# Delta-rule layer: decay exponents spread over partitions by DMA instead of matmuls, and a new order of exponentials and projections

## The chip, the cores and the metric

The kernel runs on one core of a Trainium2 chip. TensorE (matmuls), VectorE, ScalarE and GpSimd (called POOL in the profile) each run their own in-order queue of instructions; SyncE (SP) only issues transfers here. The metric is the device time of one execution in microseconds, the median of several runs.

## What is computed

An encoder trunk over 512 positions of width 1024: a gated delta-rule mixer, an MLP, a gated linear attention mixer and an MLP, each followed by a layer norm. The change lies in the first mixer alone. For each of 8 heads and both directions it does, in chunks (cut from the reference):

```python
gc = jnp.cumsum(g.reshape(bn, h, n, CHUNK), axis=-1)
decay_mat = jnp.exp(jnp.where(causal, gc[..., :, None] - gc[..., None, :], -jnp.inf))
a_mat = jnp.where(strict, jnp.einsum('bhncd,bhnsd->bhncs', kb, k) * decay_mat, 0.0)
lhs = a_mat + jnp.eye(CHUNK, dtype=F32)
sol = lax.linalg.triangular_solve(lhs, rhs, left_side=True, lower=True, unit_diagonal=True)
u, w = sol[..., :dv], sol[..., dv:]
qk = jnp.einsum('bhncd,bhnsd->bhncs', q, k) * decay_mat
q_dec = q * jnp.exp(gc)[..., None]
...
v_new = u_c - jnp.einsum('bhcd,bhde->bhce', w_c, state)
o = jnp.einsum('bhcd,bhde->bhce', qd_c, state) + jnp.einsum('bhcs,bhse->bhce', qk_c, v_new)
state = state * gl_c[..., None, None] + jnp.einsum('bhcd,bhce->bhde', kd_c, v_new)
```

Here `g` is the log decay of each position, `gc` its running sum. The matrix `decay_mat` needs, for each pair of positions, the exponential of a difference of two running sums: one varies along the partitions, the other along the free axis.

## The kernel before, in words

The kernel works in chunks of 128 positions, 4 per head (`NT`), with 2 directions, so a head has 8 matrices of 128x128. It splits float32 operands in two halves for the projections (`mm3`, lines 128 to 130: three matmuls of 512 columns per 128 rows of depth, 24 per block, four blocks k, q, v, z per head).

The layer is written as generators of one head each, `project`, `rows`, `solve`, `recur` and `finish`, and the loop in `gdn` (line 1367) runs through them: in step i it traces the recurrence of head i-2, the solve of head i-1, the projection of head i, then the finish of head i-2. The order in which they are traced gives each instruction its priority. A planner then works out the order on each engine ahead of time: it takes ready instructions by priority, with a cost for each, and gives out buffers as they come free. So the next head's projection fills the gaps of the current head's solve. `issue_after(x)` puts what follows behind x on x's engine, and `in_order` fixes an order by hand.

The steps that matter here:

- `project` (line 1423) loads and splits the weights (`wcols`, `split`, lines 102 and 107: a cast on ScalarE, a subtraction on VectorE), multiplies, and convolves on ScalarE and VectorE (`conv`, line 1408: a scaling and four shifted multiply-adds). After k and q it takes SiLU of both and calls `rows`.
- `rows` (line 1463) transposes k and q to get the norms, and forms for each position `rw`, its running log decay less half the log of k's norm (line 1488). It splits `rw` in three bfloat16 parts (1492 to 1496), transposes them in four matmuls into 6 rows (`rtp`, 1499), and copies these to SBUF (`rt`, 1501).
- `solve` (line 1519) multiplies k with itself (`kk`, 1528). Two matmuls with a 0/1 matrix `sel` (1534) put the rows, summed over their three parts, on all 128 partitions in two PSUM banks (`ep`); ScalarE takes their exponential times q (`qd`, 1536 and 1537). Two more matmuls add a triangular mask of -1e30 (`mi`, 1549) to the same banks. ScalarE takes `exp(ep + cj)`, 8 pieces per head (`E`, 1553), and VectorE multiplies by `kk` (1555). From there on the triangular inverse is built by doubling block sizes 4 to 64 (`xp`, 1585; `lv`, 1614 to 1634). The last copies of the inverse are on ScalarE (`Dd`, 1649) and VectorE (1651); a correction step and the products of `E` with q and k (`qke`, 1674) end the solve.
- `recur` (line 1687) runs through the 4 chunks of both directions and forms the output with `qd` and `qke` (1744). `finish` normalises it.
- The masks are built once at the start by POOL (`masks`, line 1170), after the gates.

SBUF tiles come from rings: `E` has two buffers of 2 KB per partition, `qd` four; PSUM has two banks for `ac` (where `ep` and all matrices of the solve go), three for `pj` (projections), two for `ch` and one for `tp`.

Of the kernel before, what the change touches and what calls it, by code (L numbers as in the profile page):

```python
# [8 lines left out]
F32 = mybir.dt.float32  # L9
# [8 lines left out]
P = 128  # L18
# [1103 lines left out]
class GdnConst:  # L1122


    def __init__(self, c, pool, w_in, w_g, a_log, dt_bias, conv_w, norm_g, x):
        self.c, self.pool = c, pool
        nc = c.nc
# [42 lines left out]
    def masks(self):  # L1170
        c, pool = self.c, self.pool
        G = c.nc.gpsimd
        self.idb = pool.tile([P, P], BF16, name="idb", bufs=1)
        G.tensor_copy(self.idb, c.ident)
        self.idh = pool.tile([P, P], F16, name="idh", bufs=1)
        G.tensor_copy(self.idh, c.ident)

        sf = pool.tile([6, 2, P], F32, name="self", tag="E", bufs=2)
        G.memset(sf, 0.0)
        for s in range(3):  # L1180
            G.affine_select(out=sf, in_=sf, compare_op=ALU.not_equal, fill=1.0, base=-2 * s,
                            pattern=[[-1, 2], [0, P]], channel_multiplier=1)
        self.sel = pool.tile([6, 2, P], BF16, name="sel", bufs=1)
        G.tensor_copy(self.sel, sf)
        self.mi = [pool.tile([P, P], BF16, name=f"mi{d}", bufs=1) for d in range(2)]
        for d in range(2):
            t = pool.tile([P, P], F32, name="tri", tag="cf", bufs=2)
            self.tri(t, d, False, 0.0, NEG)
            G.tensor_copy(self.mi[d], t)

# [146 lines left out]
def gdn(c, w_in, conv_w, a_log, dt_bias, norm_g, w_out, ln_g, ln_b, x, xt, w_next):  # L1337
    tc, nc = c.tc, c.nc
    w_in, w_g = w_in
    with c.banks(ch=2, pj=3, tp=1, ac=2), tc.tile_pool(name="gdn", bufs=1) as pool:  # L1340
        g = GdnConst(c, pool, w_in, w_g, a_log, dt_bias, conv_w, norm_g, xt)
        hi = [c.big.tile([P, 2, S], F32R, name=f"oh{t}", tag=f"xt{t}") for t in range(NT)]
# [8 lines left out]
        def load_z(hf):  # L1351
            if hf:
                tl = pool.tile([P, NT, S], F32, name="z", tag="sil", bufs=3)
            else:
                tl = heads[-1].next.kq
                more = [heads[-1].t2(tag, n).rearrange("p n i -> p (n i)") for tag, n in (("kt", 3), ("qd", 4))]
            for t in range(NT):
                z[t][hf] = tl[:, t, :] if hf or t < 2 else more[t - 2]
                c.dma(z[t][hf], x[t * P:(t + 1) * P, 512 * hf:512 * hf + 512])
# [7 lines left out]
        for i in range(A_H + 2):  # L1367
            old, mid, new = (heads[j] if 0 <= j < A_H else None for j in (i - 2, i - 1, i))
            if old:
                run(old.recur(done))  # L1370
            if mid:
                run(mid.solve(done))
            if new:
                run(new.project(done))
            if i >= A_H:
                load_z(i - A_H)
                run(c.out_pieces(w_out, early, lhs, z, "pj", (i - A_H,), 1))
            if old:
                run(old.finish(done))
# [7 lines left out]
class GdnHead:  # L1387
# [20 lines left out]
    def conv(self, a, ps, ci):  # L1408

        V, A, g = self.c.nc.vector, self.c.nc.scalar, self.g  # L1410
        A.mul(a, ps, g.cw[:, 2, ci:ci + 1])
        for k in (0, 1, 3, 4):
            d = k - 2
            lo, hi = max(0, -d), S - max(0, d)
            V.scalar_tensor_tensor(a[:, lo:hi], ps[:, lo + d:hi + d], g.cw[:, k, ci:ci + 1], a[:, lo:hi],
                                   ALU.mult, ALU.add)

    def new_tile(self):
        self.sil = self.pool.tile([P, 4, S], F32, name="sil", tag="sil", bufs=3)
        self.kq = self.sil[:, 2:4, :]  # L1420
        return self.sil[:, 0:2, :]

    def project(self, done):
# [6 lines left out]
        for i, ci in enumerate((A_H + h, h, 2 * A_H + h, 3 * A_H + h)):  # L1430
# [16 lines left out]
            if i < 3:  # L1447
                self.conv(kq[:, i, :] if i < 2 else self.v, ps, ci)
            else:
                A.copy(self.sz, ps)  # L1450
            if i == 1 or i == 3 and h == A_H - 1:
                t = vz if i == 3 else self.sil if h else kq
                c.exp_ln_after(A.activation(t, t, AF.Silu))
            yield 0.69, 0.0
            if i == 1:
                rows = self.rows(done)
                if h:
                    yield from rows
                else:
# [3 lines left out]
    def rows(self, done):  # L1463
# [20 lines left out]

        rw = c.small.tile([P, NT, 2], F32, name="rw", tag="rw")
        self.cj = cj = c.small.tile([P, NT, 2], F32, name="cj", tag="cj")
        lnk = lnr[:, 0, :].unsqueeze(2).to_broadcast([P, NT, 2])
        V.scalar_tensor_tensor(rw, lnk, -0.5, g.gc[:, :, :, h], ALU.mult, ALU.add)

        rs = c.small.tile([P, NT, 6], BF16, name="rsp", tag="rsp")  # L1490
        r1 = c.small.tile([P, NT, 2], F32, name="r1", tag="r1")
        V.tensor_copy(rs[:, :, 0:2], rw)
        V.tensor_tensor(r1, rw, rs[:, :, 0:2], ALU.subtract)
        V.tensor_copy(rs[:, :, 2:4], r1)
        V.tensor_tensor(r1, r1, rs[:, :, 2:4], ALU.subtract)
        V.tensor_copy(rs[:, :, 4:6], r1)
        rtp = self.bank("rtp", BF16, tag="tp")
        for n in range(NT):
            T.transpose(rtp[:6, n, :], rs[:, n, :], g.idb)
        self.rt = pool.tile([6, S], BF16, name="rt", tag="rt", bufs=2)  # L1500
        A.copy(self.rt, rtp[:6, :, :].rearrange("p n i -> p (n i)"))
        V.scalar_tensor_tensor(cj, lnk, -0.5, g.lg[:, :, :, h], ALU.mult, ALU.add)
# [16 lines left out]
    def solve(self, done):  # L1519
# [10 lines left out]

        eps, self.qd = [], []
        for d in range(2):
            ps = self.bank("ep")
            T.matmul(ps, g.sel[:, d, :], self.rt, start=True, stop=True)
            x = self.t2("qd", 4)
            A.activation(x, ps, AF.Exp)
            V.tensor_tensor(x, self.kq[:, 1, :].rearrange("p (n i) -> p n i", n=NT), x, ALU.mult)
            self.qd.append(x)
            eps.append(ps)
        yield 0.63, 1.4  # L1540

        ath, atl = t8("ath", 1), t8("atl", 1)
# [3 lines left out]
        ex, ats = [], []  # L1546
        with c.in_order(mybir.EngineType.PE):
            for d in (1, 0):
                T.matmul(eps[d], g.idb, g.mi[d].unsqueeze(1).to_broadcast([P, NT, P]), start=False, stop=True, skip_group_check=True)
        for d, ps in enumerate(eps):  # L1550
            e = self.t2("E", 2)
            for n in range(NT):
                A.activation(e[:, n, :], ps[:, n, :], AF.Exp, bias=self.cj[:, n, d:d + 1])
            at = kks if d else self.t2("on", 2)
# [31 lines left out]
        xd = t8("Xd", 1)  # L1586
        A.copy(xd, xp)

# [59 lines left out]
        for d in range(2):  # L1648
            A.copy(dd[row(1 - d), dirs[d], row(d)], ps[row(1 - d), d, :, :])
        for d in range(2):  # L1650
# [36 lines left out]
    def recur(self, done):  # L1687
# [52 lines left out]
        for n in (1, 2, 0, 3):  # L1740
            mm = [(self.qke[d][:, n, :], vns[d][n]) for d in range(2)]
            mm += [(self.qd[d][:, n, :], states[d][n]) for d in range(2) if states[d][n] is not None]
            for i, (l, r) in enumerate(mm):
# [102 lines left out]
```

## Time and profile before

| | |
|---|---|
| median of 3 runs | 1328.03 us (1326.8 to 1328.38) |
| the profiled execution | 1328.52 us |
| its span in the trace | 1326.6 us |
| mean granted TensorE clock | 0.997 of full |
| TensorE, VectorE, ScalarE, POOL busy | 1307.4, 1107.7, 805.2, 124.8 us |
| instructions | 22309 |

The delta-rule layer is the first of four and takes about the first 420 us. Durations of matmuls include the time in which they overlap with the next one, so two instructions of 0.39 us may start 0.23 us apart. In rows of a timeline the first column is the start from the beginning of the span, the second the duration, and equal instructions in a row are merged, with their count behind an x.

### The profile page before, as it was taken

Reading aid. Unit: us, or ns where it says so; the run is one execution under the profiler, and the core shown is the slowest. Engines: PE = TensorE matmul, PEld = TensorE weight load, DVE = VectorE, ACT = ScalarE, POOL = GpSimd, SP = SyncE. Lnnn points to the kernel's source line nnn. Section 1 sums busy time; section 2 is a strip of 40 time slices with the busy share of each in tenths; the row PEclk is TensorE's granted clock in tenths of the full one; section 3 lists DMA queues with packets and bytes.
Section 4 is the critical chain, followed back from the end, with each engine's and each line's share of the span. In section 5 each row is a group of like instructions: output and inputs, shape, how many; then the busy total and the mean of one; then the engine's idle time right before and its main releaser. Section 6 shows DMA issues by size and latency. Waiting matters only on the chain.

```text
span 1326.6 us, 22309 instructions
## 1 busy us (share of the span) xinstructions
PE 1307.4 (99%) x8659; PEld 1113.2 (84%) x8659; DVE 1107.7 (83%) x1823; ACT 805.2 (61%) x1598; POOL 124.8 (9%) x177
## 2 busy tenths in 40 slices
PE   9999999999999999999999999999999999999996
PEld 7777877787777889999998888888889889999985
DVE  7787888888668988989988787967879789989887
ACT  4757666767643666566667754654456466666656
POOL 5000000000000910101102200000001001101021
PEclk9999999999999999999999999999999999999998
DMA  5210120211222585675648521111216465657465
GB/s 181 96 49 33 49 65 33 64 49 57 73 99 85 189 178 154 156 191 153 151 150 170 149 90 64 65 63 64 95 64 213 105 193 154 149 172 161 142 143 143
DMA packets 44045, 154.36 MB, mean 116 GB/s; under 512 B 5419, under 2 KB 5795, under 8 KB 43939
## 3 DMA queue, kind: packets, MB, share of 16 engines
q1 hardware_dynamic: 32163, 110.85, 24.9%
q0 software_dynamic: 11776, 42.08, 16.1%
q8 instruction: 68, 1.11, 0.3%
q14 instruction: 38, 0.31, 0.1%
HBM read 113.99 MB, written 2.10 MB: 88 GB/s over the span
## 4 chain that ended last, share of the span: by engine, by line
PE 92%; ACT 3%; DVE 3%; issue 1%; DVEq 0%; POOL 0%; ACTq 0%; POOLq 0%
PE fx L128 3%; PE fx L130 3%; PE fx L129 3%; PE pX L130 3%; PE pX L129 3%; PE pX L128 3%; PE pjv L128 3%; PE pjv L129 3%; PE pjv L130 3%; PE m L1708 3%; PE fyz L128 3%; PE fyz L129 3%; PE fyz L130 3%; PE pY L129 2%; PE pY L128 2%; PE pY L130 2%
## 5 line engine op out<-in xcount | busy, mean ns | idle before, releaser
L102 ACT CAST wh<-wst 128x1024 fp32r<-128x1024 f32 x152 | 159.4, 1049 | 110.3 <-PE fyz L129 35.3
L107 DVE TENSOR_TENSOR wl<-wst,wh 128x1024 fp32r<-128x1024 f32 x150 | 184.3, 1229 | 42.2 <-ACT wh L102 41.9
L107 DVE TENSOR_TENSOR w2l<-w2r,w2h 128x1024 fp32r<-128x1024 f32 x92 | 112.3, 1221 | 24.0 <-ACT w2h L102 23.8
L102 ACT CAST w2h<-w2r 128x1024 fp32r<-128x1024 f32 x94 | 98.5, 1048 | 47.4 <-PE pX L130 16.2
L415 POOL DMA_DIRECT2D w2r<-w2r x56 | 48.5, 892 | 493.9 <-DVE w2l L107 247.3
L102 ACT CAST ah<-h 128x1024 fp32r<-128x1024 f32 x56 | 58.9, 1052 | 40.8 <-PE pX L129 18.1
L464 DVE TENSOR_TENSOR wst<-wst 128x512 f32<-128x512 f32 x120 | 79.8, 685 | 0.4
L107 DVE TENSOR_TENSOR al<-h,ah 128x1024 fp32r<-128x1024 f32 x56 | 68.3, 1220 | 5.1 <-ACT ah L102 4.8
L130 PE MATMUL pX<-w2h,al 128*128 128x512 f32 x168 | 66.2, 394 | 0.0
L129 PE MATMUL pX<-w2l,ah 128*128 128x512 f32 x168 | 66.1, 393 | 0.0
L128 PE MATMUL pX<-w2h,ah 128*128 128x512 f32 x168 | 65.8, 392 | 0.0
L128 PE MATMUL pjv<-wh,xth 128*128 128x512 f32 x128 | 54.7, 427 | 0.0
L128 PE MATMUL fx<-xth,wh 128*128 128x256 f32 x192 | 53.6, 279 | 0.0
L130 PE MATMUL fx<-xh,wl 128*128 128x256 f32 x192 | 53.6, 279 | 0.0
L130 PE MATMUL fyz<-xh,wl 128*128 128x256 f32 x192 | 53.6, 279 | 0.0
L128 PE MATMUL fyz<-xh,wh 128*128 128x256 f32 x192 | 53.6, 279 | 0.0
L128 PE MATMUL fx<-xh,wh 128*128 128x256 f32 x192 | 53.5, 278 | 0.0
L129 PE MATMUL fx<-xl,wh 128*128 128x256 f32 x192 | 53.5, 278 | 0.0
L130 PE MATMUL fx<-xth,wl 128*128 128x256 f32 x192 | 53.4, 278 | 0.0
L129 PE MATMUL fx<-xtl,wh 128*128 128x256 f32 x192 | 53.4, 278 | 0.0
L129 PE MATMUL fyz<-xl,wh 128*128 128x256 f32 x192 | 53.4, 278 | 0.0
L129 PE MATMUL pj<-xtl,wh 128*128 128x256 f32 (+1 forms) x160 | 52.0, 326 | 0.2 <-DVE xtl L194 0.2
(538 smaller groups left out, 4320.7 us busy)
## 6 DMA issues: line engine op xcount, KB each, us to landing
wst<-in_w SPq DMA_DIRECT2D x68, 512.0 KB, 4.3
w2r<-in_w SPq DMA_DIRECT2D x60, 512.0 KB, 4.0
w2r<-w2r POOLq DMA_DIRECT2D x56, 512.0 KB, 5.3
wst<-in_a_in SPq DMA_DIRECT2D x32, 512.0 KB, 3.3
wst<-in_b_vr SPq DMA_DIRECT2D x16, 512.0 KB, 3.3
wst<-in_a_out SPq DMA_DIRECT2D x8, 512.0 KB, 3.3
wst<-in_b_in SPq DMA_DIRECT2D x8, 512.0 KB, 3.3
wst<-in_b_out SPq DMA_DIRECT2D x8, 512.0 KB, 3.3
```

The lines of the kernel that those rows point to most:

```text
L102: h = nc.scalar.copy(hi, src)
L107: self.halves = h, nc.vector.tensor_tensor(lo, src, hi.bitcast(F32), ALU.subtract)
L128: mm(ps, ah, bh, start=start, stop=False, **kw)
L129: mm(ps, ah, bl, start=False, stop=False, **kw)
L130: self.last_mm = mm(ps, al, bh, start=False, stop=stop, **kw)
L415: nc.gpsimd.dma_start(blocks[a + (q,)], blocks[b + (q,)], accum_op=ALU.add)
L464: plus = lambda a, b: V.tensor_tensor(a, a, b, ALU.add)
L1708: T.matmul(ps[:, d, :], *ops(d), start=True, stop=True)
```

## The change

The rows are no longer spread over the partitions by matmuls. The triangular masks of both directions go to DRAM once, repeated for four chunks; for each head a transfer from SP's queue loads them into `E`. One float32 transpose turns `rw` into 8 rows of 128, a copy takes them to SBUF, a transfer from ScalarE's queue writes them to DRAM, and two transfers from POOL's queue read them back, broadcast to all partitions: one adds to `E`, one fills `qd`. ScalarE then takes both exponentials in place, from SBUF.

The exponentials of `E` are put behind a named ScalarE instruction: the last copy into `Dd` of the solve of the head before, and for head 0 the scaling at the head of head 1's q convolution. Those of `qd` come behind the copy of `xp` to `Xd`. The convolutions of k and q, SiLU and `rows` of heads 1 to 7 get a higher priority (`soon`). In step 1 of the loop the projection of head 1 is traced ahead of the solve of head 0, which gets a priority as if it began at the same point.

```diff
-    def __init__(self, c, pool, w_in, w_g, a_log, dt_bias, conv_w, norm_g, x):
+    def __init__(self, c, pool, dram, w_in, w_g, a_log, dt_bias, conv_w, norm_g, x):
...
     def masks(self):
-        self.idb = pool.tile([P, P], BF16, name="idb", bufs=1)
-        G.tensor_copy(self.idb, c.ident)
...
-        sf = pool.tile([6, 2, P], F32, name="self", tag="E", bufs=2)
-        G.memset(sf, 0.0)
-        for s in range(3):
-            G.affine_select(out=sf, in_=sf, compare_op=ALU.not_equal, fill=1.0, base=-2 * s,
-                            pattern=[[-1, 2], [0, P]], channel_multiplier=1)
-        self.sel = pool.tile([6, 2, P], BF16, name="sel", bufs=1)
-        G.tensor_copy(self.sel, sf)
-        self.mi = [pool.tile([P, P], BF16, name=f"mi{d}", bufs=1) for d in range(2)]
+        later = pool.tile([P, 2, P], F32, name="later", bufs=1)
         for d in range(2):
-            t = pool.tile([P, P], F32, name="tri", tag="cf", bufs=2)
-            self.tri(t, d, False, 0.0, NEG)
-            G.tensor_copy(self.mi[d], t)
+            self.tri(later[:, d, :], d, False, 0.0, NEG)
+        self.later = self.dram.tile([P, 2, NT, P], F32, name="laterd", bufs=1)
+        for n in range(NT):
+            G.dma_start(self.later[:, :, n, :], later)
...
+            if i == 1:
+                start = tc.cur_priority
+                run(new.project(done))
+                mid.solved = new.begun
+                with tc.high_priority(offset=tc.cur_priority - start):
+                    run(mid.solve(done))
+                continue
             if mid:
                 run(mid.solve(done))
...
+    def soon(self, n=350):
+        return self.c.tc.high_priority(offset=n) if self.h else contextlib.nullcontext()
...
             if i < 3:
-                self.conv(kq[:, i, :] if i < 2 else self.v, ps, ci)
+                with self.soon(250) if i < 2 else contextlib.nullcontext():
+                    begun = self.conv(kq[:, i, :] if i < 2 else self.v, ps, ci)
+                if i == 1:
+                    self.begun = begun
...
-                c.exp_ln_after(A.activation(t, t, AF.Silu))
+                with self.soon():
+                    c.exp_ln_after(A.activation(t, t, AF.Silu))
             yield 0.69, 0.0
             if i == 1:
+                self.e = pool.tile([P, 2, NT, P], F32, name="E", tag="E", bufs=2)
+                c.nc.sync.dma_start(self.e, g.later)
                 rows = self.rows(done)
                 if h:
-                    yield from rows
+                    with self.soon():
+                        yield from rows
...
-        rw = c.small.tile([P, NT, 2], F32, name="rw", tag="rw")
+        rdn = c.small.tile([P, 2, NT], F32, name="rw", tag="rw")
+        rw = rdn.rearrange("p d n -> p n d")
...
-        V.tensor_copy(rs[:, :, 0:2], rw)
-        V.tensor_tensor(r1, rw, rs[:, :, 0:2], ALU.subtract)
-        V.tensor_copy(rs[:, :, 2:4], r1)
-        V.tensor_tensor(r1, r1, rs[:, :, 2:4], ALU.subtract)
-        V.tensor_copy(rs[:, :, 4:6], r1)
-        rtp = self.bank("rtp", BF16, tag="tp")
-        for n in range(NT):
-            T.transpose(rtp[:6, n, :], rs[:, n, :], g.idb)
-        self.rt = pool.tile([6, S], BF16, name="rt", tag="rt", bufs=2)
-        A.copy(self.rt, rtp[:6, :, :].rearrange("p n i -> p (n i)"))
+        rtp = self.bank("rtp", shape=(2 * NT, P), tag="tp")
+        T.transpose(rtp, rdn.rearrange("p d n -> p (d n)"), c.ident)
+        rt = pool.tile([2 * NT, P], F32, name="rt", tag="rt", bufs=2)
+        A.copy(rt, rtp)
+        row = g.dram.tile([2 * NT, P], F32, name="row", tag="row", bufs=3)
+        self.qd = pool.tile([P, 2, NT, P], F32, name="qd", tag="qd", bufs=2)
+        c.nc.scalar.dma_start(row, rt)
+        every = row.rearrange("u p -> (u p)").partition_broadcast(P)
+        c.nc.gpsimd.dma_start(self.e.rearrange("p d n i -> p (d n i)"), every, accum_op=ALU.add)
+        c.nc.gpsimd.dma_start(self.qd.rearrange("p d n i -> p (d n i)"), every)
...
-        eps, self.qd = [], []
-        for d in range(2):
-            ps = self.bank("ep")
-            T.matmul(ps, g.sel[:, d, :], self.rt, start=True, stop=True)
-            x = self.t2("qd", 4)
-            A.activation(x, ps, AF.Exp)
-            V.tensor_tensor(x, self.kq[:, 1, :].rearrange("p (n i) -> p n i", n=NT), x, ALU.mult)
-            self.qd.append(x)
-            eps.append(ps)
-        yield 0.63, 1.4
...
-        with c.in_order(mybir.EngineType.PE):
-            for d in (1, 0):
-                T.matmul(eps[d], g.idb, g.mi[d].unsqueeze(1).to_broadcast([P, NT, P]), start=False, stop=True, skip_group_check=True)
-        for d, ps in enumerate(eps):
-            e = self.t2("E", 2)
-            for n in range(NT):
-                A.activation(e[:, n, :], ps[:, n, :], AF.Exp, bias=self.cj[:, n, d:d + 1])
+        for d in range(2):
+            e = self.e[:, d, :, :]
+            with c.tc.issue_after(self.solved.ins):
+                for n in range(NT):
+                    A.activation(e[:, n, :], e[:, n, :], AF.Exp, bias=self.cj[:, n, d:d + 1])
...
-        A.copy(xd, xp)
+        with c.tc.issue_after(A.copy(xd, xp).ins):
+            for d in range(2):
+                x = self.qd[:, d, :, :]
+                A.activation(x, x, AF.Exp)
+                V.tensor_tensor(x, self.kq[:, 1, :].rearrange("p (n i) -> p n i", n=NT), x, ALU.mult)
...
-            A.copy(dd[row(1 - d), dirs[d], row(d)], ps[row(1 - d), d, :, :])
+            self.next.solved = A.copy(dd[row(1 - d), dirs[d], row(d)], ps[row(1 - d), d, :, :])
```

## Rows read from the trace of the kernel before

**Rows 1.** Page, part 1: engines, busy us (share of the span) xinstructions.

```profile
PE 1307.4 (99%) x8659; PEld 1113.2 (84%) x8659; DVE 1107.7 (83%) x1823; ACT 805.2 (61%) x1598; POOL 124.8 (9%) x177
```

**Rows 2.** Table by stretches, the sum of eight stretches from 50 to 420 us.

```profile
sum 370.00, PE 366.50 PEld 288.77 DVE 300.01 ACT 233.67 POOL 2.38; mean PE 45.81 PEld 36.10 DVE 37.50 ACT 29.21 POOL 0.30
```

**Rows 3.** Timeline of TensorE, head 0: start us, us, engine, line, operation, tiles, shapes.

```profile
39.52 0.60 PE L1473 MATMUL ktp<-ident,sil 128*128 128x128 f32 x4
39.88 0.48 PE L128 MATMUL pjk<-xth,wh 128*128 128x512 f32 x1
...
43.91 0.40 PE L130 MATMUL pjk<-xth,wl 128*128 128x512 f32 x1
44.24 0.39 PE L1499 MATMUL rtp<-idb,rsp 128*6 128x128 bf16 x4
44.56 0.50 PE L128 MATMUL pjq<-xth,wh 128*128 128x512 f32 x1
44.90 0.40 PE L129 MATMUL pjq<-xtl,wh 128*128 128x512 f32 x1
...
47.05 0.60 PE L1534 MATMUL ep<-rt,sel 6*128 6x512 bf16 x2
47.58 0.50 PE L128 MATMUL pjq<-xth,wh 128*128 128x512 f32 x1
...
48.62 0.39 PE L129 MATMUL pjq<-xtl,wh 128*128 128x512 f32 x1
48.85 0.61 PE L1549 MATMUL ep<-mi,idb 128*128 128x512 bf16 x2
49.11 0.58 PE L130 MATMUL pjq<-xth,wl 128*128 128x512 f32 x1
49.52 0.39 PE L128 MATMUL pjq<-xth,wh 128*128 128x512 f32 x1
```

**Rows 4.** Groups of ScalarE, 40 to 400 us: busy, mean ns, idle before, releasers.

```profile
L102 ACT CAST wh<-wst 128x1024 fp32r<-128x1024 f32 x34 | 35.9, 1056 | 24.7 <-PE pjv L129 9.5 <-PE pjk L129 7.8 <-PE pjq L129 3.5
```

**Rows 5.** Waits of SP's queue (times, longest), transfers of line 415, transfer issues.

```profile
SPq L52 <- DVE wl L107: 251.9, 27, 23.7
...
L415 POOL DMA_DIRECT2D w2r<-w2r x56: 847/862/1245, 462.0 to 1281.4; - x56
...
DMA to landing us min/median/max: 4.5/5.1/10.3
...
out<-xt SPq DMA_DIRECT2D x4, 256.0 KB, 3.5
```

**Rows 6.** Timelines of VectorE and ScalarE, heads 1 and 4, columns as in rows 3.

```profile
71.60 0.17 DVE L1488 SCALAR_TENSOR_TENSOR rw<-lnr,gc 128x8 f32<-128x8 f32 x1 [0.48 <-ACT lnr L1481]
...
77.62 0.76 ACT L1649 CAST Dd<-lv 64x256 f16<-64x256 f32 x2
...
88.30 1.40 ACT L1553 ACTIVATE E<-ep,cj 128x128 f32<-128x128 f32 x5 [0.89 <-PE ep L1549]
...
208.27 0.16 DVE L1488 SCALAR_TENSOR_TENSOR rw<-lnr,gc 128x8 f32<-128x8 f32 x1
...
215.61 1.14 ACT L1553 ACTIVATE E<-ep,cj 128x128 f32<-128x128 f32 x4 [0.95 <-PE ep L1549]
```

**Rows 7.** The start: stretch 4 to 8 us, then timelines of POOL, ScalarE, TensorE.

```profile
4.00:8.00 4.00, 4.00 (x24) 4.00 (x23) 2.32 (x2) 2.49 (x4) 2.86 (x7) 1.00 0.97 333
...
2.83 0.20 POOL L1166 MEMSET tri<- 128x128 f32 x1
...
8.81 1.05 ACT L1242 CAST xth<-xt 128x1024 fp32r<-128x1024 f32 x1 [1.49 <-DMA xt<-in_xt]
...
11.24 0.62 PE L1266 MATMUL pjk<-xth,wh 128*128 128x512 f32 x2
```

**Rows 8.** Timeline of ScalarE, exponentials of head 0, query convolution of head 1.

```profile
49.55 2.24 ACT L1553 ACTIVATE E<-ep,cj 128x128 f32<-128x128 f32 x8 [0.99 <-PE ep L1549]
...
53.73 0.68 ACT L1411 ACTIVATE sil<-pjq,cw 128x512 f32<-128x512 f32 x1
```

More of the change, by code (lines that the diff above doesn't have):

```diff
@@ L1122 @@
 class GdnConst:
-    def __init__(self, c, pool, w_in, w_g, a_log, dt_bias, conv_w, norm_g, x):
-        self.c, self.pool = c, pool
+    def __init__(self, c, pool, dram, w_in, w_g, a_log, dt_bias, conv_w, norm_g, x):
+        self.c, self.pool, self.dram = c, pool, dram
         nc = c.nc
@@ L1339, in gdn @@
     w_in, w_g = w_in
-    with c.banks(ch=2, pj=3, tp=1, ac=2), tc.tile_pool(name="gdn", bufs=1) as pool:
-        g = GdnConst(c, pool, w_in, w_g, a_log, dt_bias, conv_w, norm_g, xt)
+    with c.banks(ch=2, pj=3, tp=1, ac=2), tc.tile_pool(name="gdn", bufs=1) as pool, \
+            tc.tile_pool(name="gdr", bufs=1, space=bass.MemoryType.DRAM) as dram:
+        g = GdnConst(c, pool, dram, w_in, w_g, a_log, dt_bias, conv_w, norm_g, xt)
         hi = [c.big.tile([P, 2, S], F32R, name=f"oh{t}", tag=f"xt{t}") for t in range(NT)]
@@ L1355, in load_z @@
                 tl = heads[-1].next.kq
-                more = [heads[-1].t2(tag, n).rearrange("p n i -> p (n i)") for tag, n in (("kt", 3), ("qd", 4))]
+                more = [heads[-1].t2("kt", 3).rearrange("p n i -> p (n i)"),
+                        pool.tile([P, 2, S], F32, name="qd", tag="qd", bufs=2)[:, 0, :]]
             for t in range(NT):
@@ L1410, in conv @@
         V, A, g = self.c.nc.vector, self.c.nc.scalar, self.g
-        A.mul(a, ps, g.cw[:, 2, ci:ci + 1])
+        begun = A.mul(a, ps, g.cw[:, 2, ci:ci + 1])
         for k in (0, 1, 3, 4):
@@ L1416, in conv @@
                                    ALU.mult, ALU.add)
+        return begun
     def new_tile(self):
@@ L1488, in rows @@
         V.scalar_tensor_tensor(rw, lnk, -0.5, g.gc[:, :, :, h], ALU.mult, ALU.add)
-        rs = c.small.tile([P, NT, 6], BF16, name="rsp", tag="rsp")
-        r1 = c.small.tile([P, NT, 2], F32, name="r1", tag="r1")
-        V.tensor_copy(rs[:, :, 0:2], rw)
-        V.tensor_tensor(r1, rw, rs[:, :, 0:2], ALU.subtract)
-        V.tensor_copy(rs[:, :, 2:4], r1)
-        V.tensor_tensor(r1, r1, rs[:, :, 2:4], ALU.subtract)
-        V.tensor_copy(rs[:, :, 4:6], r1)
-        rtp = self.bank("rtp", BF16, tag="tp")
-        for n in range(NT):
-            T.transpose(rtp[:6, n, :], rs[:, n, :], g.idb)
-        self.rt = pool.tile([6, S], BF16, name="rt", tag="rt", bufs=2)
-        A.copy(self.rt, rtp[:6, :, :].rearrange("p n i -> p (n i)"))
+        rtp = self.bank("rtp", shape=(2 * NT, P), tag="tp")
[8 more added lines that the diff above has]
+        c.nc.gpsimd.dma_start(self.qd.rearrange("p d n i -> p (d n i)"), every)
         V.scalar_tensor_tensor(cj, lnk, -0.5, g.lg[:, :, :, h], ALU.mult, ALU.add)
@@ L1741, in recur @@
             mm = [(self.qke[d][:, n, :], vns[d][n]) for d in range(2)]
-            mm += [(self.qd[d][:, n, :], states[d][n]) for d in range(2) if states[d][n] is not None]
+            mm += [(self.qd[:, d, n, :], states[d][n]) for d in range(2) if states[d][n] is not None]
             for i, (l, r) in enumerate(mm):
```

## The prediction

> **What bounds the kernel now.** I read the first part of the page, then the table by stretches, then the timelines of single heads, then the transfers. On the page TensorE is busy 99% of the span and VectorE 83% [rows 1]. That average covers four layers, and the change touches only the first, the delta-rule layer, which runs from 0 to about 420 us. So the stretches count: from 50 to 420 us TensorE is busy 366.5 of 370 us, VectorE 300, ScalarE 234 [rows 2]. TensorE's idle time in that part is 3.5 us in all. Each head's solve is a long chain over three engines, but its waits are filled with the next head's projection. What is worth time here is therefore a slot on TensorE, and a shorter chain alone is worth at most those 3.5 us. A busy TensorE may still hide small bubbles, since the ends of matmuls are modelled; so I price slots by the distance between starts, not by durations.
>
> **The change, part by part.**
>
> *TensorE work removed, per head.* Three groups go: four transposes of the split row sums (rtp), two selecting matmuls that spread them over 128 partitions (ep, line 1534), two that add the mask (ep, line 1549). An undisturbed projection matmul costs 0.23 us from start to start (48.62 to 48.85). From 43.91 to 44.90 there are two projection matmuls and the four rtp transposes: 0.99 - 0.46 = 0.53 us. The first ep pair: 47.05 to 47.58, 0.53 us (the switch back to the projection is not counted, as the kk matmuls ahead of it force one anyway). The mask pair: 48.62 to 49.52 less two projection slots, 0.90 - 0.46 = 0.44 us [rows 3]. Together 1.50 us a head, for 8 heads 12.0 us, all on the engine that sets the end.
>
> *TensorE work added.* One float32 transpose of 8 columns a head. Nearest row: four 128-wide transposes, 39.52 to 39.88, 0.09 us each [rows 3]; with a switch of 0.1 us I take 0.2, for 8 heads 1.5 us (ends 0.7 and 2.4). The stationary side is narrower, but 128 columns still stream, so nothing cheaper than 0.09 is likely.
>
> *VectorE and ScalarE.* Five small splits a head leave VectorE, and the row copy on ScalarE shrinks; ScalarE gains one transfer issue a head (at most the 0.86 us that POOL takes for one [rows 5], 7 us over 8 heads). The exponentials keep their number, reading SBUF in place of PSUM. Both engines have room beside TensorE [rows 2], so I take 0. The cover is TensorE's own backlog: the casts that prepare weights sit idle 24.7 us in the layer, mostly until a matmul frees their buffer [rows 4], so weights are ahead of TensorE. Without it, each microsecond that ScalarE stands would be TensorE's too.
>
> *The new transfers.* Each head adds a 512 KB mask load on SP's queue, a 4 KB row write on ScalarE's, and two 512 KB transfers on POOL's: an accumulating broadcast and a plain one. SP's queue holds weight loads which wait for a free buffer, up to 23.7 us [rows 5]; a mask load put behind one is late by that much, but its own buffer is free a head earlier, so I expect it ahead. POOL has nothing else in this stretch. The chain from row sums (rw) to usable E is: transpose and copy 0.6 us; row write, nearest row the 3.5 us of the output's writes to DRAM, which are far larger (ends: nothing, and 10.3, the longest landing in the row of accumulates); accumulate, 5.1 us median, 4.5 to 10.3, and of it 0.86 may be POOL's issue [rows 5]. That is 9.2 us, ends 5 and 21.
>
> Whether it fits: for head 1 rw is there at 71.6, the copy that the exponentials must now follow (line 1649 of the head before) ends at 78.4, and the exponentials ran at 88.3. With 9.2 us E would be there at 80.8: ScalarE stands about 2.5 us at its head, but the exponentials still run 7 us earlier than now. Head 4 is the tight one: rw 208.3, exponentials at 215.6; 9.2 us gives 217.5, 2 us late unless the raised priority of the key and query work brings rw forward [rows 6]. The qd exponentials move behind the Xd copy and come off this path. For both I take 0 on TensorE.
>
> The accumulate's row shows 5.1 us. The Trainium skill, DMA: Bandwidth & Descriptors, section on the anatomy of one DMA, fits software-issued transfers by 2.0 us plus bytes over 436 GB/s, an estimate of 3.2 us for 512 KB; by that the chain would be 7.3 us and the sum the same, since both lie inside the cover.
>
> *Start.* The mask is now written to DRAM by four POOL transfers. POOL reaches the mask at 2.8 us and issues at 0.86 us each, and from 4 to 8 us the transfer engines are 97% busy at 333 GB/s with the loads of x. 512 KB more at that rate is 1.6 us. x's second tile lands at 8.8 us and its product starts at 11.24, right after its split [rows 7]. Part of the 1.6 is covered by earlier loads being ahead in line: I take 1.0 us lost, ends 0 and 2.6 (1.6 plus 1.0 for the small pieces).
>
> *Head 0.* Its exponentials must follow head 1's query convolution, which starts on ScalarE at 53.7, so they begin at about 54.5 in place of 49.55 [rows 8]. Head 1's projection covers this; I take 0, with 4.9 us if the cover is gone.
>
> *Sum.* -12.0 + 1.5 + 1.0 = -9.5 us. The profiled execution is 1328.5 us (span 1326.6), 0.5 above the median 1328.0 of the runs shown; against that median 1318.5. With all ends favourable -11.3, and the 3.5 us of idle on top -14.8, so 1313; with head 0 and the start at their dear ends -3.0, 1325.
>
> **Rivals.** *The exponentials become the wait (slower).* They stand on ScalarE's in-order queue in front of weight casts, convolutions and the recurrence's scalings. As long as E lands within 16.7 us of rw (71.6 to 88.3 for head 1) the solve is no later than now. Past that point each microsecond delays a whole solve and what queues behind it. At the dear end of 21 us that is 4.3 us for each of heads 1 to 7, 30 us: 1328.0 - 9.5 + 30 = 1348.5; half way to that end 1333.5. For it: a write to DRAM and a read back of it by the next transfer has no row here, and accumulates of up to 10.3 us occur. Against it: these came in a stretch with far more traffic, and the median lies at half of that. The same page of the Trainium skill says that a transfer signals only when its last byte is confirmed in the target memory, and that this can be surprisingly long for DRAM; no row of a small write bears on it. I give this 0.18.
>
> *The gain is eaten (no change).* The start takes 2.6 us, head 0 takes 4.9, and a late mask load or standing ScalarE takes some 0.3 us a head: -12 + 1.5 + 2.6 + 4.9 + 2.4 = -0.6, so 1327.4. For it: the front has no slack [rows 7], and heads 4 and 0 are tight. 0.13. To this belongs the case that the removed slots were never the limit; with VectorE busy 300 of 370 us against TensorE's 366.5 I hold it to be small.
>
> *Forecast.* Slots on TensorE leave and the rest is covered: 0.69, own range 1313 to 1325.
>
> **How the numbers follow.** A measurement of this kernel tells about 0.2% from no change, 2.7 us. Below 1325.4 lies the forecast: 0.69. Within: 0.13. Above 1330.7: 0.18. The range runs from 1310, some 3 us below the most favourable sum for bubbles that the modelled ends hide, to 1332, which takes in the second rival and the mild end of the first.
>
> **What would show it.** Lines 1499, 1534 and 1549 leave TensorE's list, with 64 matmul records fewer and 8 transposes more. The steps between heads' exponentials shrink by some 1.3 us. Exponentials of heads 1 to 3 follow the line-1649 copy by 1 to 4 us instead of 10. TensorE's idle time from 50 to 410 us stays below 5 us. Layers two to four keep their lengths. I am wrong if ScalarE's waits show E or the accumulate for more than 2 us a head and TensorE idles behind its casts, or if the start slips by over 2 us.

## The result, and the profile after

The changed kernel takes 1333.96 us (median of 5 runs, 1331.26 to 1334.45) against 1328.38 us before: a ratio of 1.0042, 95% interval 1.0031 to 1.0053. It is slower by 5.6 us; the forecast was 1318.5. The profiled execution took 1333.96 us, with a span of 1332.2 us.

Part 1 of the page of the changed kernel answers to [rows 1]:

```profile
PE 1305.6 (98%) x8603; PEld 1118.7 (84%) x8603; DVE 1104.1 (83%) x1783; ACT 804.4 (60%) x1598; POOL 137.1 (10%) x189
```

TensorE has 56 matmul records fewer (8659 to 8603): 64 gone and 8 new, as foreseen. Yet the span is longer. The table by stretches says where. First the sum from 50 to 420 us, which answers to [rows 2], then six stretches of 5 us (columns: stretch, its length, busy time and count of PE, PEld, DVE, ACT and POOL, granted clock, DMA share, GB/s):

```profile
sum 370.00, PE 359.94 PEld 290.51 DVE 291.54 ACT 233.15 POOL 12.32; mean PE 359.94 PEld 290.51 DVE 291.54 ACT 233.15 POOL 12.32
...
100.00:105.00 5.00, 3.75 (x45) 2.85 (x44) 4.29 (x9) 4.91 (x15) 0.00 (x0) 1.00 0.62 211
105.00:110.00 5.00, 2.62 (x21) 2.05 (x21) 4.83 (x9) 1.21 (x3) 0.00 (x0) 0.92 0.28 108
110.00:115.00 5.00, 4.52 (x41) 3.92 (x39) 1.81 (x6) 1.39 (x6) 0.85 (x1) 0.50 0.58 107
115.00:120.00 5.00, 4.47 (x31) 3.93 (x32) 1.52 (x5) 2.91 (x7) 0.00 (x0) 0.50 0.00 0
120.00:125.00 5.00, 4.38 (x33) 3.83 (x30) 3.45 (x8) 0.96 (x4) 0.00 (x0) 0.50 0.02 5
125.00:130.00 5.00, 4.56 (x23) 4.26 (x22) 4.50 (x8) 2.17 (x5) 0.00 (x0) 0.53 0.00 0
```

TensorE's idle time in the layer has gone from 3.5 to 10.1 us, and 5.7 of it lies in these 30 us. After the gaps from 100 to 110 us the granted clock falls to 0.50, the 1.2 GHz level of two, and stays there to about 130 us. The 17.9 us that TensorE is busy from 110 to 130 us do the work of about 9.1 (each stretch's busy time by its clock), so 8.8 us are lost on top of the 5.7: an estimated 14.5 us in one hole.

What made the hole shows on TensorE earlier. The two timelines below are of TensorE (start, duration, engine, line, operation, tiles). The changed kernel around head 0's `kk`, the product of k with itself that opens a solve, and the first of head 0's output products (`op`), which come at the end of its recurrence:

```profile
68.33 0.27 PE L1504 MATMUL rtp<-ident,rw 128*8 128x128 f32 x1 [0.18 <-DVE rw L1501]
...
69.15 1.08 PE L1539 MATMUL kk<-sil 128*128 128x128 f32 x8
...
126.75 0.85 PE L1746 MATMUL op<-vn,qke 128*128 128x128 f32 x3
```

The kernel before, the same operations:

```profile
46.07 0.72 PE L1528 MATMUL kk<-sil 128*128 128x128 f32 x5
...
98.41 0.61 PE L1744 MATMUL op<-vn,qke 128*128 128x128 f32 x4
```

Head 0's solve starts 23 us later (69.1 against 46.1), right behind the transpose of *head 1's* rows. Its output products are 28 us later (126.8 against 98.4). By head 7 the lag of `op` is down to 6.8 us (400.2 against 393.4), close to the 5.6 us of the result: the later heads win back some 3 us each, and not all of it.

**Theory.** `kk`, the transposes of k and q (`ktp`) and of the rows (`rtp`) share the PSUM ring `tp`, which has one bank, and the buffers of a ring go out in the order in which they are traced, whatever the priority. Step 1 of the loop now traces head 1's projection, its `ktp` and `rtp` included, ahead of head 0's solve. So `kk` of head 0 must wait for head 1's rows. Head 0 then holds its `sil` buffer for longer (there are three; each takes v and z of one head and k and q of the next). The projections that run ahead fill the others, their results stay in PSUM, and TensorE runs out of places to write. The rows bear this end of it out, first TensorE, then ScalarE:

```profile
99.38 0.40 PE L130 MATMUL pjk<-xth,wl 128*128 128x512 f32 x1
...
124.10 1.20 PE L1710 MATMUL m<-sn,sil 128*128 128x128 f32 x4
...
131.76 0.47 PE L128 MATMUL pjq<-xth,wh 128*128 128x512 f32 x1
```

```profile
125.33 0.69 ACT L1412 ACTIVATE sil<-pjv,cw 128x512 f32<-128x512 f32 x1 [2.45 <-PE m L1710]
125.92 0.58 ACT L1458 COPY sil<-pjz 128x512 f32<-128x512 f32 x1
126.38 0.70 ACT L1412 ACTIVATE sil<-pjk,cw 128x512 f32<-128x512 f32 x1
```

Between 99.8 and 131.8 us TensorE does no projection at all. The product `m` of 124.10 to 125.30 is the last one of head 0's recurrence that reads k from `sil`. Right behind it, at 125.33, ScalarE starts the scaling of v that writes into a `sil` buffer, and z and k follow: three finished projections, in the three banks of `pj`, had waited for a place.

**Rivals.** The late exponentials of head 0 (the prediction's own doubtful cover); the raised priorities; transfers that come late, the prediction's first rival.

### The profile page after: what moved, and what is told of

It reads as the page before. It is cut to its first block, busy times and chain, and to the rows that moved or that the text cites. A ratio compares the mean times of both kernels' runs of the same rounds, so it can differ in the third digit from the quotient of the medians.

```text
span 1332.2 us, 22223 instructions
## 1 busy us (share of the span) xinstructions
PE 1305.6 (98%) x8603; PEld 1118.7 (84%) x8603; DVE 1104.1 (83%) x1783; ACT 804.4 (60%) x1598; POOL 137.1 (10%) x189
## 4 chain that ended last, share of the span: by engine, by line
PE 85%; DVE 6%; ACT 5%; DMA 3%; issue 1%; DVEq 0%; SPq 0%; ACTq 0%; POOLq 0%
PE m L1710 3%; PE fx L128 3%; PE fx L130 3%; PE pX L129 3%; PE pX L130 3%; PE fx L129 3%; PE pX L128 3%; PE pjv L128 3%; PE pjv L129 3%; PE pjv L130 3%; PE fyz L130 3%; PE fyz L128 3%; PE fyz L129 2%; PE pY L129 2%; PE pY L130 2%; PE pY L128 2%
```

## The experiments

Ratios are to the kernel before, run on the same chip, with 95% intervals.

**1. `kk` of head 0 ahead of the projection** (`solve` is started, and its first step traced, before the projection).

```diff
             if i == 1:
+                first = mid.solve(done)
+                next(first)
+                next(first)
                 start = tc.cur_priority
                 run(new.project(done))
...
-                    run(mid.solve(done))
+                    run(first)
```

> The changed kernel, but the product of k with itself (kk) of head 0 is traced ahead of head 1's projection; the rest of head 0's solve stays where it is. Theory A (kk shares the one tp bank with head 1's transposes, which are traced ahead of it, so head 0's solve starts 20 us late, projections run out of banks near 100 us and TensorE idles and loses clock): kk of head 0 near 46 us, the first ath copy before 60 us, no stretch with a granted clock below 1.00 before 400 us, 1317 to 1322 us. Theory B (head 0 is held by the wait of its exponentials for the transfers, and by the raised priority of head 1's rows): kk early, but the first ath copy still after 68 us, the low clock stays, 1331 to 1335 us.

Measured: 1319.6 us (1316.82 to 1320.37), ratio 0.9931 (0.9918 to 0.9944). `kk` of head 0 starts at 46.0 us again, and the stretch 50 to 420 us is:

```profile
50.00:420.00 370.00, 366.35 (x3143) 298.45 (x3141) 306.83 (x623) 236.66 (x672) 14.63 (x23) 1.00 0.31 93
```

Eight matmul records traced at another place are worth 14.4 us, and the idle time of that stretch is back at 3.65 us. Head 0's exponentials start at 55.4 us, no earlier than the 53.8 of the changed kernel, so they alone do not make the loss.

**2. Without the new order of step 1** (the branch is taken out; head 0's exponentials follow its own row copy).

```diff
-            if i == 1:
-                start = tc.cur_priority
-                run(new.project(done))
-                mid.solved = new.begun
-                with tc.high_priority(offset=tc.cur_priority - start):
-                    run(mid.solve(done))
-                continue
...
-        A.copy(rt, rtp)
+        copied = A.copy(rt, rtp)
+        if h == 0:
+            self.solved = copied
```

> The changed kernel without the branch for step 1: head 0's solve is traced ahead of head 1's projection as in the kernel before, and its exponentials come behind the copy of its own row sums. Theory A: 1317 to 1322 us, clock back to 0.997. Theory B: the exponentials of head 0 stand on ScalarE from about 46 us until E lands near 53 us, casts and convolutions behind them are late by as much, TensorE idles 3 to 6 us near 60 us: 1323 to 1330 us.

Measured: 1319.14 us (1318.02 to 1320.16), ratio 0.9934 (0.9921 to 0.9947). Here the stall that the new order seems meant to avoid is real. The table of waits, 50 to 100 us, ScalarE and TensorE (waiter, releaser: us in total, times, longest):

```profile
ACT E L1546 <- DMA E<-row: 8.6, 1, 8.6
...
PE hp L1562 <- DVE a L1551: 4.7, 1, 4.7
```

```profile
55.00:60.00 5.00, 1.66 (x8) 1.02 (x6) 2.72 (x5) 4.79 (x12) 0.00 (x0) 1.00 0.17 68
60.00:65.00 5.00, 3.69 (x26) 2.39 (x27) 3.49 (x8) 4.01 (x5) 0.00 (x0) 0.68 0.00 0
```

ScalarE stands 8.6 us before head 0's exponentials and TensorE 4.7 us behind it; the stretches, which follow, add a granted clock of 0.68 behind the gap, worth about 1.2 us of the 3.69 busy. The new order removes this stall and costs 14.8 us net (1333.96 - 1319.14).

**3. The kernel before with the new order alone.**

```diff
+            if i == 1:
+                start = tc.cur_priority
+                run(new.project(done))
+                with tc.high_priority(offset=tc.cur_priority - start):
+                    run(mid.solve(done))
+                continue
```

> The kernel before with the new order of step 1 alone: head 1's projection ahead of head 0's solve; matmuls still spread the rows and no transfer is added. Theory A: kk of head 0 comes behind head 1's rtp, TensorE idles and loses clock near 100 us, 1335 to 1345 us. Theory B: nothing here waits for a transfer, 1326 to 1331 us.

Measured: 1344.11 us (1343.13 to 1344.48), ratio 1.0121 (1.0107 to 1.0135). Without any transfer, TensorE still shows the late `kk` (first start 71.1 us in the view of the tile) and the loss:

```profile
L1534 PE MATMUL kk<-sil x24: 270/275/421, 71.1 to 115.5; 128*128 128x128 f32 x24
...
110.00:115.00 5.00, 4.02 (x21) 3.67 (x21) 3.49 (x9) 4.40 (x16) 0.00 (x0) 0.73 0.32 107
...
400.00:420.00 20.00, 13.84 (x80) 10.37 (x79) 6.27 (x21) 6.96 (x29) 0.00 (x0) 0.90 0.29 88
```

The order costs 16 us here too, where the exponentials wait for no transfer. Most of it shows at the layer's end, from 400 to 420 us: the last head, still late (`op` of its head 7 ends past 413 us), has no projection beside it.

**4. The changed kernel without raised priorities** (`soon` does nothing; the priority of head 0's solve in step 1 stays).

```diff
-        return self.c.tc.high_priority(offset=n) if self.h else contextlib.nullcontext()
+        return contextlib.nullcontext()
```

> The changed kernel with all of the raised priorities (soon) taken out, the order of step 1 kept. Theory A: kk of head 0 still stands behind head 1's transposes, since the bank is given out in the order of tracing; 1330 to 1340 us, clock below 0.995. Theory B: the raised priority was what let head 1's rows go ahead; without it 1317 to 1323 us.

Measured: 1335.71 us (1333.54 to 1336.2), ratio 1.0056 (1.0042 to 1.007). `kk` of head 0 is at 69.8 us, as the ring theory says. By the total the priorities matter little beside the bad order, but the loss lies elsewhere. The exponentials now wait for their transfer at several heads (30 to 420 us; 2.0 us in one wait in the changed kernel):

```profile
ACT E L1551 <- DMA E<-row: 14.5, 5, 4.5
```

TensorE idles 2.5 us from 260 to 265 us and 1.7 us from 350 to 355, where the changed kernel is busy for 4.90 and 5.00 us, and the hole from 100 to 115 us is smaller (2.0 us idle, and a granted clock of 0.79 and 0.52 in its last two stretches).

**5. Two rings in place of `sil`**: k with q, and v with z, in three buffers each of half the size, and SiLU in two calls.

```diff
-        self.sil = self.pool.tile([P, 4, S], F32, name="sil", tag="sil", bufs=3)
+    def pair(self, name):
+        return self.pool.tile([P, 2, S], F32, name=name, tag=name, bufs=3)
...
+                        A.activation(self.vz, self.vz, AF.Silu)
```

> The changed kernel, order of step 1 kept, but the tiles of k and q and those of v and z lie in rings of their own (3 buffers of half the size each, same room; one more SiLU call a head). Head 0's solve still begins near 70 us. Theory A (the late solve holds the buffers that head 2's v and z need, so three finished projections fill the three banks and TensorE has nothing to do): v and z of head 2 and then two more blocks can go ahead, some 10 of the 25 us without projections are filled, the stretch at low clock shrinks; 1322 to 1329 us. Rival (the gap comes from the recurrence and solve of head 0 being slow, not from full buffers): 1332 to 1336 us.

Measured: 1337.12 us (1336.83 to 1338.88), ratio 1.0071 (1.0058 to 1.0084): a miss on the time. The stretches of this kernel, and one of the groups of ScalarE's table loads at places where the changed kernel has none:

```profile
95.00:140.00 45.00, 44.45 (x423) 35.56 (x422) 35.09 (x73) 33.52 (x84) 1.40 (x2) 1.00 0.31 95
400.00:420.00 20.00, 15.38 (x75) 11.90 (x74) 6.86 (x21) 5.81 (x24) 0.00 (x0) 0.83 0.07 26
...
L1460 ACT ACT_TABLE_LOAD x7 | 9.0, 1283 | 0.4 <-ACT rt L1506 0.3
```

The hole at 100 us is gone, as it must be if full buffers made it. But the lag of head 0 stays (`kk` at 68.3 us, `op` at 123.9), and is paid in part at the layer's end, as in experiment 3. The rest of the idle time, 12 us from 50 to 400 us, lies in many other stretches: the second SiLU call also brought some 30 table loads of 1.28 us, so this run does not price the buffers by themselves.

**6. The removed matmuls twice**: the kernel before with both the selecting and the mask matmuls done two times (4 more a head; the mask is added twice).

```diff
             T.matmul(ps, g.sel[:, d, :], self.rt, start=True, stop=True)
+            T.matmul(ps, g.sel[:, d, :], self.rt, start=True, stop=True)
...
                 T.matmul(eps[d], g.idb, g.mi[d].unsqueeze(1).to_broadcast([P, NT, P]), start=False, stop=True, skip_group_check=True)
+                T.matmul(eps[d], g.idb, g.mi[d].unsqueeze(1).to_broadcast([P, NT, P]), start=False, stop=True, skip_group_check=True)
```

> The kernel before with the two spreading matmuls and the two mask matmuls of each head done twice. If TensorE's slots set the time at the price taken from the rows (0.53 + 0.44 us a head): 7.8 us more, 1335 to 1337 us. If these matmuls lie in gaps of TensorE: 1327 to 1330 us.

Measured: 1340.58 us (1339.48 to 1341.73), ratio 1.0093 (1.008 to 1.0106): 12.4 us for 32 matmuls, against the 7.8 (0.97 us a head) expected: a miss on the time. But part of it lies at the layer's end:

```profile
400.00:420.00 20.00, 18.70 (x94) 13.76 (x93) 10.52 (x25) 7.31 (x25) 0.00 (x0) 0.95 0.33 106
```

The profiled execution is 13.2 us longer than that of the kernel before (1341.73 against 1328.52). From 400 to 440 us TensorE idles 3.2 us in it (18.70 and 18.11 of 20 us busy), and the clock of 0.95 and 0.96 takes about 1.5 us more; the kernel before is busy at full clock throughout there. That leaves an estimated 8.5 us for the matmuls, near the price of the prediction.

**7. The transfers alone** (experiments 2 and 4 together: old order, no priorities).

> The spread by transfers alone: the order of step 1 and the raised priorities are both left out, head 0's exponentials come behind its own row copy, those of the other heads behind the solve ahead. Theory A (the gain comes from the slots that leave TensorE, and the priorities only keep the chain covered): 1318 to 1323 us. Rival (without priorities each head's E comes late and ScalarE stands in front of it): 1324 to 1332 us, with waits of ScalarE for the accumulate at most heads.

Measured: 1335.97 us (1333.54 to 1341.6), ratio 1.0064 (1.0049 to 1.0079). The table of waits, 30 to 420 us:

```profile
ACT E L1546 <- DMA E<-row: 20.6, 7, 7.9
...
PE m L1705 <- ACT vd L1720: 9.2, 5, 2.5
```

The time lies above both expected ranges. The waits are those of the prediction's first rival: the exponentials wait for their transfer in 7 waits, and TensorE waits for the scalings of the recurrence (`vd`) that stand behind them on ScalarE. Its condition, that `E` lands later than 16.7 us after `rw`, is not met: at head 4 `rw` comes at 204.42 us and the exponentials at 214.91, 10.5 us later. What is short is the lead: the `Dd` copy that they follow starts 2.7 us behind `rw` (207.16), against 16 us in the changed kernel. The accumulates were slower too, with a median of 6.5 us against 4.9. With the priorities (experiment 2) one such wait is left.

With the old order the priorities are worth 16.8 us; with the new one 1.8 (experiment 4). Put the other way, the new order costs 14.8 us beside the priorities and nothing without them (1335.97 and 1335.71 us). So neither part has a price of its own. Why the order costs nothing without the priorities wasn't taken apart.

**8. Experiment 1, with the mask's writes to DRAM behind the last of POOL's other masks.**

```diff
-        for n in range(NT):
-            G.dma_start(self.later[:, :, n, :], later)
...
-        G.tensor_copy(self.ic, ic[:, 0, :])
+        with c.tc.issue_after(G.tensor_copy(self.ic, ic[:, 0, :]).ins):
+            for n in range(NT):
+                G.dma_start(self.later[:, :, n, :], later)
```

> The kernel with kk of head 0 first (e1), and the four writes of the mask to DRAM moved behind POOL's last mask operation near 30 us, out of the way of the loads of x. Theory A (the writes delay the first loads by 1 to 2 us in some runs): 1315 to 1318 us, no low clock near 20 us, less spread between runs. Rival (the start has slack, the spread comes from elsewhere): 1317 to 1320 us as in e1.

Measured: 1317.49 us (1316.71 to 1318.05), ratio 0.9919 (0.9906 to 0.9932), the best of all. From 15 to 25 us, where experiment 1 had TensorE idle for 1.55 of 5 us and then a clock of 0.72, this kernel is busy for all of both stretches, at 1.00. The rows are experiment 1's:

```profile
15.00:20.00 5.00, 3.45 (x15) 2.08 (x13) 1.63 (x2) 2.62 (x4) 2.17 (x4) 1.00 0.48 194
20.00:25.00 5.00, 5.00 (x20) 3.91 (x21) 5.00 (x8) 2.31 (x5) 4.66 (x6) 0.72 0.64 220
```

But it loses about as much elsewhere: from 55 to 60 us it idles for 2.34 us, and from 60 to 65 its clock is 0.68, where experiment 1 has 0.73 us of idle time at full clock. The two profiled executions took the same time (1317.13 and 1316.93 us).

**9. The new order kept, `kk` in another ring**: the ring `ac`, with two banks.

```diff
-        kk = self.bank("kk", tag="tp")
+        kk = self.bank("kk")
```

> The changed kernel with its order kept, but head 0's kk product (as every head's) takes a bank of the ring ac (two banks) in place of the one bank of the ring tp. Ring theory: it is only the turn in the ring tp that held head 0's solve back, so kk of head 0 goes back from 69.1 us to about 46, the recurrence's first product of head 0 from 126.8 to 100-112, the stretch 100-130 us runs at granted clock 0.95 or more, and the time is 1316-1322 us. Rival (the traced order or the raised priorities themselves hold the solve back, whatever the bank): kk of head 0 stays above 60 us and the time at 1331-1336 us. Third possibility: kk now waits for a bank of ac that the mixing products hold, kk between 46 and 60, time 1322-1331 us.

Measured: 1320.72 us (1319.65 to 1321.29), ratio 0.9943 (0.993 to 0.9956). `kk` of head 0 starts at 39.2 us, `op` of head 0 at 108.8, and the hole is gone:

```profile
L1539 PE MATMUL kk<-sil x8: 271/274/276, 39.2 to 40.3; 128*128 128x128 f32 x8
...
100.00:105.00 5.00, 5.00 (x46) 4.43 (x44) 4.54 (x14) 3.22 (x13) 0.00 (x0) 1.00 0.47 149
105.00:110.00 5.00, 4.92 (x46) 4.32 (x45) 2.81 (x7) 3.98 (x11) 0.85 (x1) 1.00 0.72 168
```

Order, priorities and exponentials are those of the changed kernel; one word about a bank gives 13.2 us back. So it is the turn in the ring, and not the order or its priorities as such, that made the loss. That the planner gives out buffers as they come free, as told ahead of the prediction, is not the whole of it: whose turn it is follows the order of tracing.

**10. The new order kept, head 0's exponentials behind its own row copy.**

```diff
-                mid.solved = new.begun
...
-        A.copy(rt, rtp)
+        copied = A.copy(rt, rtp)
+        if h == 0:
+            self.solved = copied
```

> The changed kernel with its order kept, but head 0's exponentials follow head 0's own row copy in place of head 1's query convolution. Ring theory: where the exponentials stand doesn't matter, since kk of head 0 still waits for its turn; kk of head 0 stays near 69 us and the time at 1331-1337 us. Rival (the exponentials queued behind head 1's query copy are what delays head 0): the recurrence's first product of head 0 goes from 126.8 to below 115 us and the time is 1317-1325 us.

Measured: 1327.81 us (1326.97 to 1329.52), ratio 0.9999 (0.9991 to 1.0008). Both sides miss. `kk` of head 0 is as late as ever (75.0 us) and `op` at 125.4, as the ring theory says; but the time is 6 us below the changed kernel, though the exponentials start no earlier (56.0 us against 53.8). TensorE's lost time is in other places:

```profile
55.00:60.00 5.00, 3.81 (x17) 2.76 (x15) 2.85 (x4) 3.96 (x10) 0.00 (x0) 1.00 0.34 119
60.00:65.00 5.00, 1.52 (x6) 1.43 (x7) 1.28 (x2) 4.74 (x4) 0.00 (x0) 0.76 0.29 105
65.00:70.00 5.00, 5.00 (x15) 3.90 (x14) 3.29 (x4) 2.63 (x9) 0.00 (x0) 0.56 0.05 8
110.00:115.00 5.00, 4.23 (x34) 3.07 (x34) 4.99 (x13) 4.72 (x15) 0.85 (x1) 1.00 0.32 106
115.00:120.00 5.00, 3.98 (x42) 3.26 (x42) 3.52 (x10) 1.71 (x7) 0.00 (x0) 1.00 0.91 203
120.00:125.00 5.00, 4.01 (x49) 3.29 (x49) 4.21 (x11) 3.50 (x9) 0.00 (x0) 1.00 0.32 116
```

The hole after 110 us costs 2.8 us of idle time at full clock, in place of 14.5. Ahead of it, ScalarE now stands 8.7 us for `E`, which costs TensorE 4.7 us of idle time and, by the clocks of 60 to 70 us, 2.6 more. Against experiment 2, which differs from this run in the order alone, the late solve costs 8.7 us here. It is dear either way; how dear depends on whether its gaps bring the low clock. Why the clock stayed up after 110 us in this run wasn't taken apart.

**11. Experiments 9 and 8 together** (`kk` in `ac`, late writes).

> The changed kernel with kk in the ring ac, and the four mask writes to DRAM issued behind POOL's last mask copy in place of ahead of the other masks. Ring theory, with the start's share as seen in the run with the late write (1317.5 against 1319.6 us): 1314-1320 us, with no gap over 1 us of TensorE between 4 and 20 us. Rival (ring ac is no better a place than a full start): 1320-1327 us.

Measured: 1320.02 us (1317.34 to 1322.85), ratio 0.9941 (0.9929 to 0.9953). The time lies on the border of the two expected ranges. No gain over experiment 9 that these runs can tell; the place of the writes is worth at most 2 us, and the runs leave open whether it is worth anything.

In one row, by the medians (each step beside those above it; in another order the steps cost otherwise, as experiments 4 and 7 show):

```
before                                      1328
transfers alone (7)                         1336
 + raised priorities (2)                    1319
 + new order of step 1 (the change)         1334
 + kk of head 0 traced first (1)            1320
 + mask writes late (8)                     1317
```

## Why the prediction was wrong

**The step that failed** is the one on head 0: "Its exponentials must follow head 1's query convolution [...] Head 1's projection covers this; I take 0, with 4.9 us if the cover is gone." It saw one effect of the new order, the delayed exponentials, and that part was small: they start at 53.80 us, 4.25 us later than in [rows 8], and in experiments 1 and 9 at 55.4 and 54.4, without the loss. It did not follow the rest of what the moved step issues. The projection that was traced ahead takes its turns in the rings, and the ring `tp` of one bank, which the prediction's account of buffers (`E`, weights) never listed, puts `kk` behind head 1's rows. In place of 0 to 4.9 us the new order cost 14.8 us net, beside the priorities. The hole at 100 us, an estimated 14.5 us, was 5.7 us of idle time and 8.8 of the halved clock; the stall at head 0 that the order took away goes against it. The "own range 1313 to 1325" had no term for it.

**The cover** was argued from TensorE's backlog [rows 4]: projections always at hand. That holds while buffers for their results are free. With head 0 late by 28 us they are not: the last projection matmul before the hole starts at 99.38 us. Of the signs that the prediction named, the idle time was the one that told: 10.1 us from 50 to 410 us, where less than 5 was forecast. Neither sign of being wrong came up, no wait of over 2 us a head for `E` and no later start.

**What came out right, in part by luck.** The sum of the rest: with the new order out or mended, the kernel runs at 1317.5 to 1320.7 us, against the 1318.5 forecast (-12.0 + 1.5 + 1.0 from 1328.0). But errors offset each other in it. Experiment 2 loses 4.7 us of idle time and 1.2 by the clock from 55 to 65 us, where the kernel before is busy at full clock, and the sum took this at nothing. Its profiled execution is 9.4 us shorter than that of the kernel before (1319.14 against 1328.52), so by estimate some 15 us were saved elsewhere, against the 10.5 of the slots (-12.0 + 1.5). In experiment 9 the same estimate gives 10.4 (7.6 us shorter, with 6.25 us idle from 50 to 420 us against 3.5). So the runs leave the worth of the slots between some 10 and 15 us.

Two terms inside the sum were off in small ways. An added transpose costs 0.11 us rather than 0.2: in this timeline of TensorE it and one projection matmul, which starts at 43.73, take 0.34 us from start to start, less 0.23. The switch of 0.1 us that the prediction added came from no row, and doesn't show.

```profile
43.70 0.27 PE L1504 MATMUL rtp<-ident,rw 128*8 128x128 f32 x1
...
44.04 0.39 PE L128 MATMUL pjk<-xth,wh 128*128 128x512 f32 x1
```

And the start did not slip in the changed kernel (the q projection starts at 18.00 us against 18.19), where 1.0 us was taken; in experiment 1 there is a gap at 15 to 20 us, and the place of the writes settles between 0 and about 2 us.

**The chain from `rw` to `E`**, estimated at 9.2 us: for head 0 it took 10.8, from 43.01 to 53.80 us. The rows of ScalarE, its queue and POOL of the changed kernel:

```profile
44.30 0.55 ACTq L1509 DMA_DIRECT2D row<-rt  x1
...
48.86 0.94 POOL L1511 DMA_DIRECT2D E<-row  x1 [19.12 <-DMA row<-rt]
...
53.80 0.40 ACT L1551 ACTIVATE E<-E,cj 128x128 f32<-128x128 f32 x1 [2.01 <-DMA E<-row]
```

The write was issued 1.3 us after `rw` (0.6 taken for transpose and copy), the 4 KB write took 4.6 us until POOL could go on (3.5 taken), the accumulate 4.9 (5.1 taken). For heads 1 to 7 the cover held: this wait is the only one of ScalarE for `E`. The answer to [rows 6], head 1's timeline of ScalarE, then head 4's of VectorE and ScalarE:

```profile
101.55 0.76 ACT L1651 CAST Dd<-lv 64x256 f16<-64x256 f32 x2
102.21 2.44 ACT L1551 ACTIVATE E<-E,cj 128x128 f32<-128x128 f32 x8
...
206.65 0.18 DVE L1501 SCALAR_TENSOR_TENSOR rw<-lnr,gc 128x8 f32<-128x8 f32 x1
...
222.73 0.36 ACT L1651 CAST Dd<-lv 64x256 f16<-64x256 f32 x1
223.00 1.28 ACT L1551 ACTIVATE E<-E,cj 128x128 f32<-128x128 f32 x4
```

Both heads' exponentials come right behind the `Dd` copy that they were told to follow, 0.3 to 0.7 us after its start, sooner than the 1 to 4 us forecast for heads 1 to 3; head 4, held to be tight, has 16 us from `rw`.

**The rivals.** "The exponentials become the wait" gave its side of the outcome but not its mechanism: in the changed kernel it is 2.0 us at head 0. Its waits are real without the priorities (experiment 7), where its mild price of 1333.5 is close to the 1336 measured, but not under its condition: from `rw` to the exponentials it was 8 to 12 us, and `rw` came too close to the copy that they follow. The prediction mentioned the priorities once, as something that may bring head 4's `rw` forward; with the old order they were worth 16.8 us. The layers behind kept their length: the lag of 6.8 us at head 7 is about the loss in the end.

## What to carry to other kernels

Where a step is traced earlier, list every buffer that it takes, ring by ring, and ask who stood in that ring behind it; a ring of one bank turns a change of order into a dependence that no instruction shows. Price a late producer twice: what waits for it, and which buffers it keeps from those that run ahead, since a cover of work at hand ends when their outputs have no place to go. When a change has several parts, split them early, and run the combinations: here the priorities gained 17 us in the old order and 2 in the new, the order lost 15 us beside the priorities and nothing without them, and both would have been misjudged from the whole.

## What the hardware showed that was not expected

- A hole of a few microseconds cost more by the clock (8.8 us) than by itself (5.7). After gaps of 1.25 and 2.38 us in two neighbouring stretches of 5 us, the granted clock was 0.50 for 15 us and 0.53 for 5 more. A float32 product `m` of 128x128 took 456 to 480 ns there, as the groups by line from 110 to 128 us show, against 278 to 293 ns at full clock in experiment 9 (96 to 112 us):

```profile
L1710 PE MATMUL m<-r,xf 128*128 128x128 f32 x12 | 4.2, 480 | 0.4 <-DVE r L1717 0.4
```

```profile
L1710 PE MATMUL m<-r,xf 128*128 128x128 f32 x12 | 2.0, 278 | 0.0
```

- In experiment 10, idle time of 0.77, 1.02 and 0.99 us in three neighbouring stretches of 5 us came with a granted clock of 1.00 throughout.
- Of two transfers of the same 512 KB from the same 4 KB source on POOL's queue, the accumulating one landed sooner after its issue than the plain one. The plain one is always issued second (49.48 against 48.86 us at head 0), so it may have stood behind the first; no run tells the kind from the place. The page's transfer issues (KB each, median us to landing):

```profile
E<-row POOLq DMA_DIRECT2D x8, 512.0 KB, 4.9
qd<-row POOLq DMA_DIRECT2D x8, 512.0 KB, 6.3
```

The accumulate's 4.9 us stands against the estimate of 3.2 us that the prediction worked out from the Trainium skill, DMA: Bandwidth & Descriptors, section on the anatomy of one DMA; the trace decides, and bears out the 5.1 us that the sum took.
